# Where the large SBUF tiles of a two-layer encoder kernel begin: a 1696-byte filler, and one small tile moved to another pool

## The chip, the cores and the metric

The program runs on one core of a Trainium2 chip. The metric is device time in microseconds (us): the kernel before takes 2171.83 us, the median of three runs (2171.77 to 2172.46). A core has TensorE (PE in the profile; its weight loads are shown apart, as PEld), VectorE (DVE), ScalarE (ACT), GpSimd (POOL) and SyncE (SP), which here only issues DMAs. SBUF is the on-chip memory that all of them read; a tile of SBUF has 128 partitions, and its place is an address within each partition. This change is about that address.

## The reference

An encoder trunk of two layers over one sequence of 256 tokens and 2048 channels, in float32. Each layer is a token mixer and a gated feed-forward block, each behind an RMSNorm with gain, and with shift, scale and gate from a conditioning vector c:

```python
mod = silu(c) @ w_ada[i] + b_ada[i]          # 6 x 2048 values per layer: sh1 sc1 gt1 sh2 sc2 gt2
h = rmsnorm(x, g_norm[i, 0]) * (1 + sc1) + sh1
x = x + gt1 * (gmlp(h) if i == 0 else gqa(h))
h = rmsnorm(x, g_norm[i, 1]) * (1 + sc2) + sh2
x = x + gt2 * conv_ffn(h)                    # 2048 -> 2 x 5632 -> three-tap conv, gelu gate -> 2048
out = rmsnorm(x, g_final)
```

The gMLP mixer multiplies h by a 2048 x 4096 matrix, mixes tokens in chunks of 128 and multiplies by 2048 x 2048. The attention mixer has 16 query heads and 4 key/value heads of width 128, with a norm of each head and rotary positions.

## The kernel before

All activations lie transposed: 128 channels on the partitions, the 256 tokens along the row, 16 blocks of channels. Weights come from HBM in pieces of mostly 128 x 2048 float32 (1 MB), and every product is made from two parts of each factor, a rounded one and its remainder, both of type float32r: `weight` (L175) loads a piece into a `raw` tile, ScalarE writes the rounded part `hi` (L185), VectorE the remainder `lo` (L186), in chunks of 1024 columns. Activations are split alike: `make_h` (L267) writes the normed input as `hhi` and `hlo`, and `split_f` (L280) writes each 256-token block of an inner activation as `fhi` and `flo`. A product of a 128 x 128 weight block with a 128 x 256 activation block is then three matmuls (`prod_b`, L204), and the third partner, lo times lo, is left out:

```python
mm(out, whi, xhi, start, False)      # mm: T.matmul(out, lhsT=weight, rhs=activation), L202
mm(out, whi, xlo, False, False)
mm(out, wlo, xhi, False, stop)
```

The first operand is the stationary one, loaded into the array by a weight load before each matmul, the second is the moving one, streamed through. In the feed-forward up products (PSUM tiles `pfa`, `pfc`, `pf`) and in the u half of the gMLP (`pu`) the moving operand is a 256-column slice of `hhi` or `hlo`; in the down products (`pd`) and in the output products of the mixers (`po`, `pw`) it is a tile `fhi` or `flo`. Three products have the roles the other way round: in `pv`, `pk` and `pq` 128 columns of `hhi` or `hlo` are stationary and 512 columns of `hi` or `lo` are moving.

Between these, VectorE also makes the 192 columns of `mod` (`ada`, L133: a 1 MB piece of w_ada times a broadcast of silu(c), summed along the row), as the function `pump` hands them out with the weights. `rstd_bcast` (L237) makes 1/rms at the start of each of the five norms, with a small tile `r` of two values per partition. The Tile framework orders the instructions by priority and sets the semaphores; each pool reuses its buffers in turn, and an instruction that writes a reused buffer waits for the last reader.

Pools are laid out one behind the other in the order in which they are opened (L60 to L65): `const` (single small tiles, x, cond_bc), `raws` (5 x 8192 bytes per partition), `his` and `los` (5 x 4096 each), `hbuf` (`hhi` and `hlo`, 16384 each), `tmp` (`ht` 2 x 1024, `acc` 2048, `sqj` 2048, `r` 2 x 32), and, opened anew for each mixer, the pool of `fhi` and `flo` (1024 each) and a scratch pool. A tile takes at least 32 bytes and is padded to a multiple of 32. The const pool begins 128 bytes past a multiple of 1024 (the framework's own constants) and is 30,784 bytes long, so that `raws` begins at 192 past a multiple of 1024. Since all tiles from there to `tmp` are multiples of 1024, all of raw, hi, lo, hhi and hlo begin at 192 past a multiple of 1024 too; the two buffers of r add 64, and fhi and flo begin at 256 past one. Slices of 128 columns are 512 bytes, those of 256 columns 1024 bytes.

Of the kernel before, what the change touches and what calls it, by code (L numbers as in the profile page):

```python
# [9 lines left out]
F32 = mybir.dt.float32  # L10
# [5 lines left out]
P = 128  # L16
# [3 lines left out]
TC = S // P  # L20
# [18 lines left out]
RB = 5  # L39
FB = 18  # L40
HW = 1024
PARTS = (16, 16, 12)
SH1, SC1, GT1, SH2, SC2, GT2 = range(6)

# [2 lines left out]
def kernel(  # L47
# [10 lines left out]
    V, A, G, T, Q = nc.vector, nc.scalar, nc.gpsimd, nc.tensor, nc.sync  # L58

    const = ctx.enter_context(tc.tile_pool(name="const", bufs=1))  # L60
# [8 lines left out]
        return cur["ps"].tile([P, 512], F32, tag=tag or cur["tag"], name=name, bufs=cur["bufs"][tag or cur["tag"]])  # L69

    def phase(stack, name, nf, bufs={"ps": 8}, tag="ps", rt="ps"):
        """pools that live for one mixer: PSUM banks, split activations, scratch"""
        cur["ps"] = stack.enter_context(tc.tile_pool(name=name + "_ps", bufs=1,
                                                     space=bass.MemoryType.PSUM, reuse_waits="tile"))
        cur["bufs"], cur["tag"], cur["rt"] = bufs, tag, rt
        cur["f"] = stack.enter_context(tc.tile_pool(name=name + "_f", bufs=nf, reuse_waits="tile"))
        cur["scr"] = stack.enter_context(tc.tile_pool(name=name, bufs=1, reuse_waits="tile"))
        return cur["scr"]
# [1 line left out]
    def raw_tile(name):  # L80
        return raws.tile([P, 2048], F32, tag="raw", name=name)

# [1 line left out]
    def small(name, shape, src=None):  # L84
        t = const.tile(shape, F32, tag=name, name=name)
        if src is not None:
            Q.dma_start(t, src)
        return t
# [19 lines left out]
    mod = small("mod", [P, DEPTH, 6 * NB])  # L108
    gs = small("gs", [P, DEPTH * 2, NB])

# [1 line left out]
    cond = small("cond", [P, NB])  # L112
    A.activation(cond, cT, AF.Exp, scale=-1.0)
    V.tensor_scalar(out=cond, in0=cond, scalar1=1.0, scalar2=None, op0=ALU.add)
    V.reciprocal(cond, cond)
    V.tensor_tensor(out=cond, in0=cond, in1=cT, op=ALU.mult)
    cond_bc = small("cond_bc", [P, D])
    c_st = ExitStack()
    cur["ps"] = c_st.enter_context(tc.tile_pool(name="c_ps", bufs=2, space=bass.MemoryType.PSUM, reuse_waits="tile"))
    cur["tag"], cur["bufs"] = "ps", {"ps": 2}  # L120
# [8 lines left out]
        A.copy(cond_bc[:, b * S:(b + 1) * S], pb[:, :S])  # L129
    c_st.close()  # L130

# [1 line left out]
    def ada(l, vec, j):  # L133
        m = vec * NB + j
        w = raw_tile(f"ada{l}_{m}")
# [21 lines left out]
        while it not in done:  # L157
            pump_one()

# [1 line left out]
    cnt = [0]  # L161
    pend = []

# [43 lines left out]
        mm(out, whi, xlo, False, False)  # L207
        mm(out, wlo, xhi, False, stop)

# [1 line left out]
    accs = {}  # L211

    def square_into(name, j, src):
# [1 line left out]
            square_(name, j, src)  # L215

    def square_(name, j, src):
        """sum of squares over the blocks of x, two blocks at a time; the last block goes to the tensor engine"""
        if j < NB - 2 and j % 2 == 0:
            return  # L220
        if j < NB - 2:
            src, n = x[:, j - 1:j + 1, :].rearrange("p j t -> p (j t)"), 2 * S
        else:
            n = S
        if j == 1:
            accs[name] = tmp.tile([P, 2 * S], F32, tag="acc", name=f"acc_{name}", bufs=1)
            A.activation(accs[name], src, AF.Square)
            return
        s = tmp.tile([P, 2 * S], F32, tag="sqj", name=f"sq_{name}{j}", bufs=SQB)[:, :n]
        A.activation(s, src, AF.Square)  # L230
        if j < NB - 1:
            V.tensor_tensor(out=accs[name][:, :n], in0=accs[name][:, :n], in1=s, op=ALU.add)
        else:
            a = accs[name]
            accs[name] = (a[:, S:], a[:, :S], s)

    def rstd_bcast(name, keep):  # L237
        """1 / rms of every token over all partitions: a PSUM tile, and a copy in SBUF if it is kept for long"""
        pm = bank(f"pm_{name}", cur["rt"])
        r = tmp.tile([P, TC], F32, tag="r", name=f"r_{name}")  # L240
        dg = tmp.tile([P, S], F32, tag="ht", name=f"dg_{name}")
        pr = bank(f"pr_{name}", cur["rt"])
        for i, a in enumerate(accs[name]):
            for t in range(TC):
                T.matmul(pm[:, t:t + 1], lhsT=a[:, t * P:(t + 1) * P], rhs=mean_w, start=i == 0 and t == 0,
                         stop=i == 2, skip_group_check=True)
        with tc.high_priority():
            V.tensor_scalar(out=r, in0=pm[:, :TC], scalar1=EPS, scalar2=None, op0=ALU.add)
            G.tensor_tensor(out=r, in0=r, in1=neghalf[:, :TC], op=ALU.pow)
            for t in range(TC):  # L250
                V.tensor_scalar(out=dg[:, t * P:(t + 1) * P], in0=ident, scalar1=r[:, t:t + 1],
                                scalar2=None, op0=ALU.mult)
                T.matmul(pr[:, t * P:(t + 1) * P], lhsT=ones, rhs=dg[:, t * P:(t + 1) * P], start=True, stop=True)
            if not keep:
                return pr[:, :S]
            R = cur["scr"].tile([P, S], F32, tag="R", name=f"R_{name}", bufs=1)
            A.copy(R, pr[:, :S])
        return R
# [32 lines left out]
            V.scalar_tensor_tensor(out=x[:, j, :], in0=src, scalar=mcol(l, vec, j), in1=x[:, j, :],  # L291
                                   op0=ALU.mult, op1=ALU.add)

# [1 line left out]
    def gmlp(l, rstd):  # L295
        with ExitStack() as st:
            gm = phase(st, "gm", NB)
# [87 lines left out]
    def gqa(l, rstd):  # L385
        with ExitStack() as st:
# [28 lines left out]
                        mm(pk[t][n], hlo[:, kb, ts_], w(n * 512, 512)[0], False, kb == NB - 1)  # L415

            def rope(nm, ps2, cs):
                """un-normalised rotation of four heads and 1/rms of each; ps2: banks per t-chunk"""
                ss = at.tile([P, TC * 4], F32, tag="qss", name=f"ss{cs}", bufs=2)
                rot = [at.tile([P, 512], F32, tag="p", name=f"rot{cs}{t}", bufs=PB) for t in range(TC)]  # L420
                for t in range(TC):
                    src = ps2[t]
                    for h in range(4):
                        s = at.tile([P, P], F32, tag="qsq", name=f"qsq{cs}{t}{h}", bufs=2)
                        A.activation(s, src[:, h * P:(h + 1) * P], AF.Square,
                                     accum_out=ss[:, t * 4 + h:t * 4 + h + 1])
                    s4 = src.rearrange("p (h d) -> p h d", h=4)
                    V.tensor_tensor(out=rot[t].rearrange("p (h d) -> p h d", h=4), in0=s4,
                                    in1=tabs[nm + "c"][:, t:t + 1, :].broadcast_to([P, 4, P]), op=ALU.mult)
                    sw = at.tile([P, 512], F32, tag="sw", name=f"sw{cs}{t}", bufs=1)  # L430
                    s5 = src.rearrange("p (h a c f) -> p h a c f", h=4, a=2, c=2)
                    sw5 = sw.rearrange("p (h a c f) -> p h a c f", h=4, a=2, c=2)
                    t5 = tabs[nm + "s"][:, t, :].rearrange("p (a c f) -> p a c f", a=2, c=2)
                    for c in range(2):
                        V.tensor_tensor(out=sw5[:, :, :, c, :], in0=s5[:, :, :, 1 - c, :],
                                        in1=t5[:, :, c, :].unsqueeze(1).broadcast_to([P, 4, 2, 32]), op=ALU.mult)
                    V.tensor_tensor(out=rot[t], in0=rot[t], in1=sw, op=ALU.add)
                V.tensor_scalar(out=ss, in0=ss, scalar1=1.0 / P, scalar2=EPS, op0=ALU.mult, op1=ALU.add)
                G.tensor_tensor(out=ss, in0=ss, in1=neghalf, op=ALU.pow)
                return rot, ss  # L440
# [110 lines left out]
    def ffn(l, rstd, nxt, defer):  # L551
        with ExitStack() as st:
# [7 lines left out]
                return b[:, :S], b[:, S:]  # L560

            def epilogue(i, src):
                """three-tap convolution along the tokens of both halves, then gelu(g) * val, split"""
                t = ff.tile([P, 2 * S], F32, tag="t", name=f"t{l}_{i}", bufs=2)
                cols = (i, NPAIR + i)
                for a, o, n in zip(src, halves(t), cols):
                    A.activation(o, a, AF.Identity, bias=cb[:, l, n:n + 1], scale=cw[:, l, 1, n:n + 1])
                for tap, frm, to in ((0, slice(0, S - 1), slice(1, S)), (2, slice(1, S), slice(0, S - 1))):
                    for a, o, n in zip(src, halves(t), cols):
                        V.scalar_tensor_tensor(out=o[:, to], in0=a[:, frm], scalar=cw[:, l, tap, n:n + 1],  # L570
                                               in1=o[:, to], op0=ALU.mult, op1=ALU.add)
                A.activation(t[:, :S], t[:, :S], AF.Gelu)
                V.tensor_tensor(out=t[:, :S], in0=t[:, :S], in1=t[:, S:], op=ALU.mult)
                return split_f(f"f{l}_{i}", t[:, :S])
# [126 lines left out]


def _cols(a, *lead):
    """(..., n*128) -> [128, ..., n]"""
    n = a.shape[-1] // P
    a = a.reshape(*a.shape[:-1], n, P)
    return np.moveaxis(a, -1, 0)


def _nblock(w):  # L710
    """(K, N) -> [N/128][128 k][K/128, 128 n]: the blocks of one column block side by side"""
    K, N = w.shape
    return w.reshape(K // P, P, N // P, P).transpose(2, 1, 0, 3).reshape(N // P, P, -1)

# [75 lines left out]
```

## Time and profile before

| what | before |
|---|---|
| median of 3 runs | 2171.83 us |
| profiled execution, first to last instruction | 2173.2 us |
| instructions | 39151 |
| PE busy | 2099.9 us (97%), 16328 matmuls |
| DVE busy | 1706.8 us (79%) |
| ACT busy | 1019.5 us (47%) |
| POOL busy | 16.6 us (1%) |
| DMA | 580.62 MB, mean 267 GB/s |
| mean granted TensorE clock | 0.980 |

The profiled execution's own time is its span, 2173.2 us. Busy time of an engine is the union of its instructions' times; matmuls overlap each other, so the duration of one (280 ns) is not what it costs: that is the distance from one start to the next. A busy PE of 97% therefore says that PE seldom waits, not that each matmul takes as little as it could.

### The profile page before, as it was taken

To read this page: it belongs to the slowest core of one execution; us is meant where nothing else is said; L and a number is where in the kernel's file an instruction comes from. 1 tells how busy PE (TensorE), PEld (TensorE's weight loads), DVE (VectorE), ACT (ScalarE), POOL (GpSimd) and SP (SyncE) were. 2 spreads that over 40 slices of the span, in tenths; PEclk is the share of its full clock that TensorE was granted. 3 is DMA by queue.
4 is the path that set the end of the run, shared out by engine and by line. 5 is a ranking of instruction groups with operands and counts; after the bars stand their busy time and mean duration, and the time that the engine had idled before them with its cause. 6 is when DMAs were issued, how large, how long until landed. Compare 5 with 4: busy or idle time off the path is not lost.

```text
span 2173.2 us, 39151 instructions
## 1 busy us (share of the span) xinstructions
PE 2099.9 (97%) x16328; PEld 2037.8 (94%) x16328; DVE 1706.8 (79%) x2291; ACT 1019.5 (47%) x1501; POOL 16.6 (1%) x15
## 2 busy tenths in 40 slices
PE   6889998999999999999999999899999999999997
PEld 4669998999999999999988789899999999999997
DVE  8989888889988989889985677876978566655665
ACT  3343444446544554345455554443653445434542
POOL 0000000000000000000000000000000000000000
PEclk7999999999999999999999999899999999999999
DMA  9999997885798889988976346677558655555542
GB/s 370 405 376 360 343 335 275 338 356 201 282 356 326 324 327 336 335 324 309 338 251 224 119 177 242 218 272 296 192 179 320 229 184 178 192 181 188 174 159 95
DMA packets 85137, 580.62 MB, mean 267 GB/s; under 512 B 9952, under 2 KB 11488, under 8 KB 25056
## 3 DMA queue, kind: packets, MB, share of 16 engines
q1 hardware_dynamic: 84960, 578.12, 71.6%
q8 instruction: 128, 2.10, 0.4%
q14 instruction: 49, 0.40, 0.1%
HBM read 575.99 MB, written 2.10 MB: 266 GB/s over the span
## 4 chain that ended last, share of the span: by engine, by line
PE 54%; issue 36%; DVE 7%; ACT 1%; DMA 1%; POOL 0%; SPq 0%; POOLq 0%; DVEq 0%; ACTq 0%
PE pf L202 18%; PE pd L202 11%; PE po L202 4%; PE pu L202 4%; PE pfc L202 4%; DVE ada L137 4%; PE pw L202 3%; PE pk L202 3%; PE pq L202 3%; DVE lo L186 2%; PE pfa L202 2%; PE pqo L506 1%; PE psc L477 0%; DMA ada<-in_wada 0%; ACT hi L185 0%
## 5 line engine op out<-in xcount | busy, mean ns | idle before, releaser
L185 ACT CAST hi<-w 128x1024 fp32r<-128x1024 f32 x740 | 740.1, 1008 | 929.9 <-PE pf L202 360.7
L186 DVE TENSOR_TENSOR lo<-w,hi 128x1024 fp32r<-128x1024 f32 x740 | 859.6, 1170 | 358.6 <-ACT hi L185 353.1
L202 PE MATMUL pf<-hhi_f,lo 128*128 128x256 f32 x2144 | 606.8, 283 | 0.0
L202 PE MATMUL pf<-hhi_f,hi 128*128 128x256 f32 x2144 | 606.8, 283 | 0.0
L202 PE MATMUL pf<-hlo_f,hi 128*128 128x256 f32 x2144 | 606.8, 283 | 0.0
L137 DVE CUSTOM_DVE_ANT_0 ada<-ada,cond_bc,bada 128x2048 f32<-128x2048 f32 x192 | 449.3, 2346 | 24.2 <-DMA ada<-in_wada 24.0
L202 PEld LDWEIGHTS pf<-hhi_f,hi 128*128 128x128 f32 x2144 | 411.6, 192 | 0.0
L202 PEld LDWEIGHTS pf<-hhi_f,lo 128*128 128x128 f32 x2144 | 411.6, 192 | 0.0
L202 PEld LDWEIGHTS pf<-hlo_f,hi 128*128 128x128 f32 x2144 | 411.6, 192 | 0.0
L202 PE MATMUL pd<-fhi_f,hi 128*128 128x256 f32 x1408 | 392.1, 280 | 0.0
L202 PE MATMUL pd<-flo_f,hi 128*128 128x256 f32 x1408 | 391.6, 279 | 0.0
L202 PE MATMUL pd<-fhi_f,lo 128*128 128x256 f32 x1408 | 391.2, 279 | 0.0
L202 PEld LDWEIGHTS pd<-fhi_f,lo 128*128 128x128 f32 x1408 | 264.1, 188 | 0.0
L202 PEld LDWEIGHTS pd<-fhi_f,hi 128*128 128x128 f32 x1408 | 263.6, 188 | 0.0
L202 PEld LDWEIGHTS pd<-flo_f,hi 128*128 128x128 f32 x1408 | 263.1, 187 | 0.0
L202 PE MATMUL pfc<-hhi_f,hi 128*128 128x256 f32 x448 | 126.1, 283 | 0.0
L202 PE MATMUL pfc<-hlo_f,hi 128*128 128x256 f32 x448 | 126.1, 283 | 0.0
L202 PE MATMUL pfc<-hhi_f,lo 128*128 128x256 f32 x448 | 125.5, 283 | 0.0
L570 DVE SCALAR_TENSOR_TENSOR t<-pf,cw,t 128x255 f32<-128x255 f32 x240 | 101.7, 474 | 0.0
L202 PEld LDWEIGHTS pfc<-hhi_f,hi 128*128 128x128 f32 x448 | 85.8, 192 | 0.0
L202 PEld LDWEIGHTS pfc<-hlo_f,hi 128*128 128x128 f32 x448 | 85.8, 192 | 0.0
L202 PEld LDWEIGHTS pfc<-hhi_f,lo 128*128 128x128 f32 x448 | 85.4, 192 | 0.0
(187 smaller groups left out, 2844.6 us busy)
## 6 DMA issues: line engine op xcount, KB each, us to landing
ada<-in_wada SPq DMA_DIRECT2D x192, 1024.0 KB, 6.6
w<-in_wup SPq DMA_DIRECT2D x134, 1024.0 KB, 4.8
w<-in_wdn SPq DMA_DIRECT2D x64, 1024.0 KB, 4.9
w<-in_wup SPq DMA_DIRECT2D x48, 896.0 KB, 5.5
w<-in_wdn SPq DMA_DIRECT2D x32, 768.0 KB, 4.7
w<-in_wv SPq DMA_DIRECT2D x16, 1024.0 KB, 7.1
w<-in_wu SPq DMA_DIRECT2D x16, 1024.0 KB, 7.1
w<-in_wout SPq DMA_DIRECT2D x16, 1024.0 KB, 5.3
```

The source lines that it names most:

```text
L137: V.tensor_tensor_reduce(out=w, in0=w, in1=cond_bc, op0=ALU.mult, op1=ALU.add, scale=1.0, scalar=bada[:, l, m:m + 1], accum_out=mod[:, l, ...
L185: A.copy(hi[:, :n], w[:, c:c + n])
L186: V.tensor_tensor(out=lo[:, :n], in0=w[:, c:c + n], in1=hi[:, :n].bitcast(F32), op=ALU.subtract)
L202: T.matmul(out, lhsT=a, rhs=b, start=start, stop=stop, skip_group_check=True)
L506: T.matmul(po, lhsT=va[:, kc, g * P:(g + 1) * P], rhs=ps_[h][:, kc, :], start=kc == 0, stop=kc == TC - 1)
L570: V.scalar_tensor_tensor(out=o[:, to], in0=a[:, frm], scalar=cw[:, l, tap, n:n + 1], in1=o[:, to], op0=ALU.mult, op1=ALU.add)
```

## The change

A tile `filler` of 424 float32 (1696 bytes) is added at the end of the const pool, of which one column is set to zero by VectorE, since a tile must be written. The tile `r` of each of the five norms goes from the pool `tmp`, where two buffers were used in turn, to the const pool, as five tiles of their own. Nothing else that is executed changes; docstrings and comment lines are left blank.

```diff
@@ -39,6 +39,7 @@
 HW = 1024
+FILL = 424
 PARTS = (16, 16, 12)
...
@@ -108,13 +109,15 @@
     cond_bc = small("cond_bc", [P, D])
+    filler = small("filler", [P, FILL])
+    V.memset(filler[:, 0:1], 0.0)
     c_st = ExitStack()
...
@@ -235,9 +238,9 @@
         pm = bank(f"pm_{name}", cur["rt"])
-        r = tmp.tile([P, TC], F32, tag="r", name=f"r_{name}")
+        r = const.tile([P, TC], F32, tag=f"r_{name}", name=f"r_{name}")
         dg = tmp.tile([P, S], F32, tag="ht", name=f"dg_{name}")
```

The const pool becomes 30,784 + 1696 + 5 x 32 = 32,640 bytes long; with the 128 bytes ahead of it that is 32 x 1024, and `raws`, `his`, `los` and `hbuf` begin at multiples of 1024. `tmp` is now 2048 + 2048 + 2048 bytes, and so `fhi` and `flo` begin at multiples of 1024 as well.

## Rows read from the trace of the kernel before

**Rows 1.** The page, engines: busy us (share of the span) and number of instructions
```profile
PE 2099.9 (97%) x16328; PEld 2037.8 (94%) x16328; DVE 1706.8 (79%) x2291; ACT 1019.5 (47%) x1501; POOL 16.6 (1%) x15
```
**Rows 2.** Windows: span, busy us (instructions) of PE, PEld, DVE, ACT, POOL, clock, DMA
```profile
27.00:145.00 118.00, 99.39 (x374) 75.24 (x375) 117.46 (x140) 40.50 (x50) 0.00 (x0) 0.90 1.01 403
161.00:250.00 89.00, 86.55 (x719) 85.85 (x718) 83.77 (x105) 39.22 (x59) 0.00 (x0) 1.00 0.89 351
651.00:835.00 184.00, 184.00 (x1535) 184.00 (x1535) 165.84 (x216) 91.23 (x125) 0.00 (x0) 1.00 0.87 324
1041.00:1105.00 64.00, 64.00 (x546) 64.00 (x545) 61.42 (x83) 30.08 (x42) 0.00 (x0) 1.00 0.94 355
```
**Rows 3.** Chain that ended last, in order of time, 165 to 1110 us: start, us, what
```profile
171.52 80.95 PE pu L202 x672
252.47 87.52 PE po L202 x743
...
474.71 86.40 PE pf L202 x720
561.11 90.45 PE pd L202 x768
651.56 184.32 PE pf L202 x1536
```
**Rows 4.** Groups by line and shape: count, busy us, mean ns; one of each three
```profile
L202 PE MATMUL pf<-hhi_f,hi 128*128 128x256 f32 x2144 | 606.8, 283 | 0.0
L202 PE MATMUL pd<-fhi_f,hi 128*128 128x256 f32 x1408 | 392.1, 280 | 0.0
L202 PE MATMUL pfc<-hhi_f,hi 128*128 128x256 f32 x448 | 126.1, 283 | 0.0
L202 PE MATMUL pw<-fhi_o,hi 128*128 128x256 f32 x256 | 72.5, 283 | 0.0
L202 PE MATMUL pu<-hhi_a,hi 128*128 128x256 f32 x256 | 72.4, 283 | 1.5 <-DVE v L367 1.5
L202 PE MATMUL po<-fhi_y,hi 128*128 128x256 f32 x256 | 71.6, 280 | 0.0
L202 PE MATMUL pfa<-hhi_f,hi 128*128 128x256 f32 x224 | 63.7, 295 | 5.2 <-ACT hhi_f L276 5.2
L202 PE MATMUL pv<-hi,hhi_a 128*128 128x512 f32 x128 | 50.8, 450 | 16.5 <-ACT hhi_a L276 16.2
L202 PE MATMUL pk<-hi,hhi_b 128*128 128x512 f32 x96 | 38.7, 403 | 1.1 <-ACT hhi_b L276 1.1
L202 PE MATMUL pq<-hi,hhi_b 128*128 128x512 f32 x96 | 38.9, 407 | 2.3 <-ACT qsqq L425 2.3
L202 PEld LDWEIGHTS pf<-hhi_f,hi 128*128 128x128 f32 x2144 | 411.6, 192 | 0.0
L202 PEld LDWEIGHTS pd<-fhi_f,hi 128*128 128x128 f32 x1408 | 263.6, 188 | 0.0
```
**Rows 5.** Timeline of PE at full clock, two matmuls nine apart: start, us, what
```profile
1139.33 0.39 PE L202 MATMUL pk<-hi,hlo_b 128*128 128x512 f32 x1
...
1141.37 0.39 PE L202 MATMUL pk<-hi,hlo_b 128*128 128x512 f32 x1
```
**Rows 6.** Timeline of PE at half clock, and the window's clock
```profile
144.08 0.63 PE L202 MATMUL pv<-lo,hhi_a 128*128 128x512 f32 x1
...
144.93 0.63 PE L202 MATMUL pv<-lo,hhi_a 128*128 128x512 f32 x1
...
144.00:145.50 1.50, 1.50 (x5) 1.13 (x4) 1.50 (x1) 1.48 (x2) 0.00 (x0) 0.50 0.99 415
```
**Rows 7.** Timeline, 13 merged 128-column float32 matmuls, a weight load each
```profile
161.82 1.61 PE L365 MATMUL pg<-ws,v 128*128 128x128 f32 x13
```
**Rows 8.** Groups by line: the small instructions that the change touches or resembles
```profile
L105 DVE MEMSET mean_w<- 128x1 f32 x1 | 0.1, 59 | 0.0
L249 POOL TENSOR_TENSOR r_ff<-r_ff,neghalf 128x2 f32<-128x2 f32 x2 | 3.4, 1714 | 291.8 <-DVE r_ff L248 291.8
```

## The prediction

> **What bounds the kernel now.** I read the engines' shares first, then the chain that ended last, then the windows. PE is busy 97% of the span [rows 1], and in the long stretches of the two feed-forward blocks it is busy all the time, with no idle time in front of its matmuls [rows 2, 4]. The exception is the first product, `pv` (27 to 145 us), where VectorE is busy 117.46 of 118 us and PE 99.39 [rows 2]. Elsewhere VectorE follows closely in the first layer: 165.84 of 184 us, 83.77 of 89, 61.42 of 64 [rows 2]. So outside `pv` time is the number of matmuls times the distance from one start to the next, and that distance is what a change of address could move.
>
> The chain gives this distance, since it merges back-to-back matmuls. 720 of `pf` take 86.40 us, 1536 take 184.32 us: 120.00 ns each, both times. 768 of `pd` take 90.45 us: 117.77 ns each. 743 of `po` take 87.52 us: 117.79 ns; `pu` is near `pf`, 80.95 us for 672 = 120.46, a few stalls included [rows 3]. All four have the same shape, 128 x 256 against a 128 x 128 weight block, and all their weights come from hi and lo. What differs is the moving operand: hhi or hlo, which begin at 192 past a multiple of 1024 bytes, in `pf` and `pu`; fhi or flo, which begin at 256 past one, in `pd` and `po`. The groups show the same split: a matmul of `pf` or `pfc` lasts 283 ns with a weight load of 192 ns, one of `pd` or `po` 280 ns with 188 ns [rows 4].
>
> For the 512-column matmuls the two starts 1139.33 and 1141.37 are nine matmuls apart: 2.04 / 9 = 226.7 ns [rows 5]. At half clock two starts lie two matmuls apart, 144.08 to 144.93: 425 ns for 512 columns, so 212.5 at full clock with nothing added, and 106 for 256 columns [rows 6]. I use 213.3 and 106.7, 512 and 256 columns at 2.4 GHz. What a matmul takes beyond its columns is then 13.3 ns in `pf`, 13.4 ns in `pk`, 11.1 ns in `pd`. It is the same for 256 and for 512 columns, so it belongs to the start of a matmul (or to its weight load) and not to the stream. At the stream's own pace (1024 bytes in 106.7 ns, 9.6 bytes per ns) 13.3 ns is the time of 128 bytes: as if a stream that begins 64 bytes past a multiple of 128 (192 is one) had to read one unit of 128 bytes more, 9 in place of 8, 17 in place of 16. 9 x 13.33 = 120.0 and 17 x 13.33 = 226.7 are the measured distances. For `pd`, which begins at a multiple of 128, 8 units would be 106.7; it takes 117.8, so something else limits it, and that other limit would show in `pf` as soon as the extra unit is gone. This is the reading that I forecast by. It rests on two start addresses and is not forced by them.
>
> **The change part by part.**
>
> The filler's memset is one more VectorE instruction; the like one on `mean_w` takes 59 ns [rows 8]. It costs between 0 and 0.06 us once. I take 0.
>
> The five r tiles of their own remove a wait for the buffer's last reader two norms earlier, long past; POOL's power on r takes 1.7 us before and after [rows 8]. Nothing comes or goes: 0. No DMA, queue or wait is added, and the order of the large work has no reason to change; were the scheduler to order a few instructions differently at the norms, I would expect tenths of a us of either sign.
>
> VectorE, ScalarE and the DMAs read and write the same shapes at other addresses. For them no row before shows a start other than 192 or 256 for the large tiles, so the bounds are a gain or loss of a few ns on each of 740 splits per engine; it is hidden by PE except in `pv` with its 32 pairs of splits, where 5 ns each would be 0.2 us. I take 0.
>
> The moving slices of hhi and hlo (`pf` 3 x 2144, `pfc` 3 x 448, `pfa` 3 x 224, `pu` 3 x 256 = 9216 matmuls [rows 4]) go from 192 to 0 past 1024. Bounds: the column time 106.7 ns below (a gain of 13.3 x 9216 = 123 us), 120.0 above if nothing is won; a loss here would need 0 to be worse than 192. The nearest row is `pd`, 117.77 ns, a start at a multiple of 128. I take that: 2.23 ns x 9216 = 20.6 us. Some 50 of them run at half clock at the start of the feed-forward blocks (`pfa` lasts 295 rather than 283 ns on the mean [rows 4]), where the extra disappears: 20.4 us.
>
> The moving tiles fhi and flo (`pd` 3 x 1408, `po` and `pw` 3 x 256 each = 5760) go from 256 to 0. Bounds: 106.7 ns below (64 us gained), 120.0 above (12.8 us lost, the second rival). I take 117.77 as before: 0.
>
> The 960 matmuls of 512 columns (`pv` 384, `pk` and `pq` 288 each [rows 4]) get an aligned stream too: at most 2.2 ns each if their extra falls from 13.3 to 11.1, nothing in `pv`, which VectorE bounds, and little of `pq`, which waits on the attention. 0.6 us.
>
> The stationary blocks go from 64 past a multiple of 128 to a multiple of 128. Nothing before shows such a weight load beside such a stream. Bounds: the other 11.1 ns of each matmul (the third rival) and a loss as in the second. I take 0.
>
> Sum: 20.4 + 0.6 = 21.0 us off the profiled execution's 2173.2 us, 2152.2. The median of the runs is 1.4 us below the profiled execution, so 2150.8 us. VectorE doesn't become the bound: `pf` from 651 to 835 us would shrink to 180.6 us, with 165.84 of VectorE's work in it.
>
> **Where a page says otherwise.** The distance at full clock is 120.0, 117.77 and 226.7 ns [rows 3, 5]. The Trainium skill, "TensorE: Matmul & The Clock Gate", section "Back-to-back issue gap", puts the gap of a single matmul at N / 2.4 + 2.5 ns: an estimate of 109 ns for 256 columns and 216 ns for 512. The trace disagrees by 9 to 11 ns per matmul; if the addresses were all that stands between the two, the sum by the page's figure would be an estimate of 149 us less (10.8 x 9216 + 8.6 x 5760 ns), which the third rival below holds in the terms of a row.
>
> **The rivals.**
>
> *Slower: the distance between the two addresses counts, not each one's alignment.* In `pf`, `pu` and `pk` the stationary and the moving operand both begin at 192 past 1024 (the stationary ones also at 704), so they lie a multiple of 512 bytes apart, and all three pay 13.3 ns. In `pd` and `po` the moving one lies 64 bytes further, and they pay 11.1 ns. If weight load and stream, which run side by side, get into each other's way when they lie a multiple of 512 apart, the change takes the 64 bytes away, and `pd`, `po` and `pw` fall to 120.0 ns: 2.23 x 5760 = 12.8 us, of which some 0.2 in `pw` lie beside waits on the attention. It decides from the first `po` on: 2171.8 + 12.6 = 2184.4 us. For it speaks that it explains the rows with no second limit, and that the weight load is 4 ns longer where the matmul is slower [rows 4]; against it, that 13.3 ns being just 128 bytes of stream is then chance.
>
> *No change: neither address counts.* The 2.23 ns would come from something that the filler leaves alone, such as hhi being slices of one large tile and fhi tiles of their own, or which part of SBUF they lie in. Then 2171.9 us. That the change doesn't do what it says comes to the same time, but the sum of the pool's tiles gives 32 x 1024 exactly. Against it: `pu` and `pf`, and `po` and `pd`, agree within each pair over different mixers. The Trainium skill says the like: "SBUF — State Buffer", section "Who interferes with whom", has PE read stationary and moving operands through two ports of its own and wait for nobody, and its "Specifications (TRN2)" give lines of 16 bytes, which both kernels' starts respect. By it the four products would not differ, and they do [rows 3].
>
> *Much faster: the rest of the extra is an alignment's price too,* of the stationary blocks, which are off by 64 bytes in every product shown. The nearest floor is `pg`: its 13 matmuls of 128 columns, bound by a weight load each, lie (1.61 - 0.28) / 12 = 111 ns apart [rows 7]. At 111 ns: 9 x 9216 + 6.8 x 5760 = 122 us, with some 3 us more from `pk` and `pq`, and some 5 us lost where VectorE has less room than that [rows 2], in `pu` and the last `pd` of layer 0: about 120 us, 2052 us. Half of it, 2112 us, is as likely as all. Against it: the weight load of `pd` is not shown waiting, and 188 ns is the shortest of the groups.
>
> **How the numbers follow.** Forecast 0.37, the slower rival 0.35, much faster 0.16, no change 0.12. Faster by over 0.2% (4.3 us, about what a measurement can tell from no change): 0.37 + 0.16 = 0.53; within 0.2%: 0.12; slower: 0.35. The forecast alone would be 2146 to 2157 us (the 512-column term from 0 to 2 us, a few us for what starting addresses of 0 do to fhi and flo). The range takes in the slower rival with 3 us for `pk` and `pq`, up to 2188, and the weaker half of the much faster one, down to 2112; about 0.1 is left out.
>
> **What would show it.** In the chain the 720 matmuls of `pf` take 84.8 us instead of 86.40, with weight loads of 188 ns, and 768 of `pd` stay at 90.45. If `pd` grows to 92.2 with weight loads of 192 ns while `pf` stays, the slower rival holds; if both stand still, the address is not it; if both fall towards 80 and 85 us, it is the weights' alignment. A different order of the instructions at the norms, or a stretch where VectorE is now waited for, would make the sum wrong without touching these.

## The result: slower, by the amount of the first rival

The changed kernel takes 2184.64 us, the median of four runs (2184.05 to 2187.21), beside 2172.14 us for the kernel before on the same chip (2171.77 to 2172.68): a ratio over the runs of 1.0061, with a 95% interval of 1.0047 to 1.0076. The forecast was 2150.8 us; the first rival, *the distance between the two addresses counts*, had put it at 2184.4. The profiled execution took 2185.03 us, of which 2183.3 from first to last instruction.

In the chain of the kernel after, in order of time (start, us, what), these are the pieces that answer to [rows 3]:

```profile
168.84 80.95 PE pu L205 x672
249.79 89.17 PE po L205 x743
...
474.25 86.40 PE pf L205 x720
560.64 92.16 PE pd L205 x768
652.80 184.32 PE pf L205 x1536
```

`pf` takes 86.40 us for 720, to the hundredth what it took before, and `pu` 80.95 for 672. `po` went from 87.52 to 89.17 for 743, `pd` from 90.45 to 92.16 for 768: both are now 120.0 ns from start to start, like `pf`. The attention's output product, which [rows 3] don't show, follows: in the chain of before 434 of `pw` from 1318.59 us take 51.13 us, 117.8 ns each; after, 554 of them take 120.0.

```profile
1318.59 51.13 PE pw L202 x434
```

```profile
1323.00 66.48 PE pw L205 x554
```

The groups of the page after, by line and shape (count, busy us and mean ns of one, idle before), answer to [rows 1] and [rows 4]:

```profile
PE 2109.7 (97%) x16328; PEld 2048.0 (94%) x16328; DVE 1706.7 (78%) x2292; ACT 1018.6 (47%) x1501; POOL 16.6 (1%) x15
...
L205 PE MATMUL pf<-hhi_f,hi 128*128 128x256 f32 x2144 | 606.8, 283 | 0.0
...
L205 PEld LDWEIGHTS pf<-hhi_f,hi 128*128 128x128 f32 x2144 | 411.6, 192 | 0.0
...
L205 PE MATMUL pd<-fhi_f,hi 128*128 128x256 f32 x1408 | 396.4, 283 | 0.0
...
L205 PEld LDWEIGHTS pd<-fhi_f,hi 128*128 128x128 f32 x1408 | 269.6, 192 | 0.0
```

A matmul of `pd` lasts 283 ns instead of 280 and its weight load 192 instead of 188; the rows of `pf` are the same to the last digit. VectorE has one instruction more and 0.1 us less to do, and the instructions of PE, ScalarE, POOL and the DMA queue stand in the same order as before. So nothing was waited for that was not waited for before: 5760 matmuls began 2.23 ns later after each other, 12.8 us. The medians differ by 12.5.

The two profiled spans differ by only 10.1 us. The other 2.7 us lie ahead of all this: `pu` begins at 168.84 us after and at 171.52 before [rows 3]. That start lies between 168.86 and 170.70 us in five of the six further chains shown below (in the sixth, with 64 bytes ahead of all four, `pu` is interrupted there), in no order that goes with an address; in `pv`, which runs until then, the granted clock was a little higher (0.92 from 27 to 145 us, [rows 2] have 0.90). So the profiled execution of before was a long one for its kernel: wherever both are on record, a run's time is 1.6 to 2.0 us above its span from first to last instruction, so that the median of 2172.14 us goes with a span of some 2170.3 us and not of 2173.2.

### The profile page after: what moved, and what is told of

Same layout as the page of the kernel before. It is cut to its first block, busy times and chain, and to the rows that moved or that the text cites. A ratio compares the mean times of both kernels' runs of the same rounds, so it can differ in the third digit from the quotient of the medians.

```text
span 2183.3 us, 39151 instructions
## 1 busy us (share of the span) xinstructions
PE 2109.7 (97%) x16328; PEld 2048.0 (94%) x16328; DVE 1706.7 (78%) x2292; ACT 1018.6 (47%) x1501; POOL 16.6 (1%) x15
## 4 chain that ended last, share of the span: by engine, by line
PE 55%; issue 36%; DVE 7%; ACT 1%; POOL 0%; DMA 0%; SPq 0%; POOLq 0%; DVEq 0%; ACTq 0%
PE pf L205 18%; PE pd L205 11%; PE po L205 4%; PE pw L205 4%; PE pu L205 4%; PE pfc L205 4%; DVE ada L140 3%; PE pk L205 3%; PE pq L205 3%; DVE lo L189 2%; PE pfa L205 2%; PE pqo L509 1%; PE psc L480 0%; PE psc L502 0%; ACT hi L188 0%
## 5 line engine op out<-in xcount | busy, mean ns | idle before, releaser
L205 PE MATMUL pd<-flo_f,hi 128*128 128x256 f32 x1408 | 397.2, 283 | 0.0
L205 PE MATMUL pd<-fhi_f,lo 128*128 128x256 f32 x1408 | 396.9, 283 | 0.0
L205 PEld LDWEIGHTS pd<-flo_f,hi 128*128 128x128 f32 x1408 | 270.0, 192 | 0.0
L205 PEld LDWEIGHTS pd<-fhi_f,lo 128*128 128x128 f32 x1408 | 269.8, 192 | 0.0
L205 PEld LDWEIGHTS pd<-fhi_f,hi 128*128 128x128 f32 x1408 | 269.6, 192 | 0.0
```

Source lines behind the costliest of these rows:

```text
L205: T.matmul(out, lhsT=a, rhs=b, start=start, stop=stop, skip_group_check=True)
```

## The experiments

The theory on trial is now the rival's: what counts is how far the moving operand lies from the weight block, and the address of neither by itself. d stands below for the address of the moving operand less that of the weight block, in bytes and with whole multiples of 256 left off (the fourth experiment shows that they don't count). Before, d is 0 in `pf`, `pfc`, `pfa`, `pu` and 64 in `pd`, `po`, `pw`; after, it is 0 in all. Against it stand: the filler (weights and hhi now at other places), the alignment of fhi and flo by itself, and the move of `r` by some way other than the 64 bytes that it gave up.

One more rival can be settled by the two traces alone: that the moving operand meets not PE's own weight load but VectorE, ScalarE or a DMA, which fill `hi`, `lo` and `raw` meanwhile. In stretches in which VectorE and ScalarE are idle for over nine tenths of the distance from one start to the next and no DMA packet is under way, before has 121 distances of `pf` with a mean of 120.0 ns and 90 of `pd` with 117.8; after has 127 and 116, all of 120. These are the means of the whole products (worked out from the traces' records), so none of those three makes the difference; what is left is PE's own two operands.

**64 bytes ahead of fhi and flo alone.** To the changed kernel:

```diff
     tmp = ctx.enter_context(tc.tile_pool(name="tmp", bufs=2))
+    fpad = tmp.tile([P, 16], F32, tag="fpad", name="fpad", bufs=1)
+    V.memset(fpad[:, 0:1], 0.0)
```

> The changed kernel with 64 bytes of pad ahead of the tiles fhi and flo alone: they begin at 64 past a multiple of 1024, weights and hhi, hlo stay at 0. Distance theory (a matmul costs 120.0 ns when its moving operand lies a multiple of 512 bytes from the weight blocks, 117.8 when it lies 64 further): pd, po and pw go back to 117.8 ns, pf stays at 120.0; 12.7 us off the changed kernel's 2184.6, so 2171.9 us, level with the kernel before. Alignment theory (that of the forecast, a start off a multiple of 128 costs): fhi and flo are now off it, so pd is at 120.0 or worse, 2184.6 us or more.

Measured: 2170.84 us, 0.9994 of the kernel before (0.9985 to 1.0004). The chain of this kernel:

```profile
473.89 86.40 PE pf L207 x720
560.29 90.45 PE pd L207 x768
```

The whole loss is gone, with `pd` back at 90.45 us, and `pf` untouched. (In this kernel's profile some 600 matmuls of `pw` and 356 of `pd` are faster still, by 4.4 ns each or 4.2 us, for a reason that the last section takes up; why the median nevertheless lies only 1.3 us below that of before I can't place.) fhi and flo begin at 64 past a multiple of 1024 here and at 256 past one before: other alignments, the same d of 64, the same 117.77 ns.

**64 bytes ahead of hhi and hlo alone.** The filler is cut to 296 floats, so that weights begin 512 bytes earlier; `hpad` of 16 floats stands ahead of hhi, and 112 floats ahead of fhi bring that one back to a multiple of 512:

```diff
-FILL = 424
+FILL = 296
...
     hbuf = ctx.enter_context(tc.tile_pool(name="hbuf", bufs=1))
+    hpad = hbuf.tile([P, 16], F32, tag="hpad", name="hpad")
+    V.memset(hpad[:, 0:1], 0.0)
     tmp = ctx.enter_context(tc.tile_pool(name="tmp", bufs=2))
+    fpad = tmp.tile([P, 112], F32, tag="fpad", name="fpad", bufs=1)
+    V.memset(fpad[:, 0:1], 0.0)
```

> The changed kernel with hhi and hlo alone 64 bytes further than a multiple of 512 from weights and fhi, flo (which stay at a multiple of 512; the filler is 512 bytes shorter to make room). Distance theory: pf, pfc, pfa and pu fall from 120.0 to 117.8 ns, 720 of pf in 84.8 us, pd stays at 120.0; 9216 x 2.23 = 20.5 us off 2184.6, so 2164 us. The products pk, pq, pv with hhi, hlo as the stationary operand move by at most 2 us. Alignment theory: pf stays at 120.0 or gets worse, 2184.6 us or more.

Measured: 2167.61 us, 0.9978 (0.9969 to 0.9988). The two products have changed places, in the chain and in the weight loads:

```profile
472.84 84.80 PE pf L209 x720
557.64 92.17 PE pd L209 x768
649.80 180.91 PE pf L209 x1536
...
1119.81 59.97 PE pk L209 x257
```

```profile
L209 PEld LDWEIGHTS pf<-hhi_f,hi 128*128 128x128 f32 x2144 | 402.3, 188 | 0.0
...
L209 PEld LDWEIGHTS pd<-flo_f,hi 128*128 128x128 f32 x1408 | 270.0, 192 | 0.0
```

180.91 us for 1536 is 117.78 ns. This is the 84.8 us in `pf` that the prediction had hoped for, and it comes from taking hhi *off* the alignment. What is dearer than I had expected is `pk`: 59.97 us for 257 is 233.3 ns where it was 226.7 [rows 5]. There the roles are the other way round (hhi is the weight block, d is -64), and the 64 bytes cost 6.7 ns for 512 columns. On the 576 matmuls of `pk` and `pq` that is at most 3.8 us, and the measured time is 3.6 us above the expected 2164. (`pv`, the third product of this kind, goes to 233 ns as well, where VectorE and not PE sets the time.)

**64 bytes ahead of all four.** The changed kernel with `hpad` alone, which shifts fhi and flo as well:

```diff
     hbuf = ctx.enter_context(tc.tile_pool(name="hbuf", bufs=1))
+    hpad = hbuf.tile([P, 16], F32, tag="hpad", name="hpad")
+    V.memset(hpad[:, 0:1], 0.0)
```

> The changed kernel with hhi, hlo, fhi and flo all 64 bytes further than a multiple of 1024 from the weights. Distance theory: both gains, 2184.6 - 12.7 - 20.5 = 2151.4 us, 1.0% below the kernel before; if the gains do not add up, another engine (VectorE in the first layer) is the bound. Alignment theory: 2184.6 us or more.

Measured: 2152.94 us, 0.9911 (0.9895 to 0.9927). In its chain both products are at 117.8 ns, and `pk` at 233.3 (53.67 us for 230):

```profile
469.89 84.80 PE pf L207 x720
554.69 90.45 PE pd L207 x768
...
1119.96 53.67 PE pk L207 x230
```

The two gains add up (the dearer `pk` and `pq` and some 600 faster matmuls of `pw`, 2.7 us, nearly cancel), and this is near the forecast's time, reached by the opposite address: 64 past a multiple of 1024 for everything that I had wanted at 0.

**A row of distances in one kernel.** The filler at 296 floats again, and rows of hhi and hlo 8 floats longer, so that block kb lies 32 bytes further from its weights than the one before:

```diff
-        hts["hi"] = hbuf.tile([P, NB, S], F32R, tag="hhi", name=f"hhi_{name}")
+        hts["hi"] = hbuf.tile([P, NB, S + 8], F32R, tag="hhi", name=f"hhi_{name}")[:, :, :S]
```

and the same for hlo.

> A map in one run: the rows of hhi and hlo are 1056 bytes instead of 1024, so that block kb begins 32 x kb bytes past a multiple of 512 from the weights, for kb 0 to 15; fhi and flo stay at a multiple of 512. Distance theory: within each group of pf, pfc and pu the distance from start to start varies with kb, 120.0 at kb 0 and 117.8 at kb 2 (64 bytes), and takes other values elsewhere; the curve over 0 to 480 bytes tells whether 64 is the best distance. Alignment theory: 117.8 or less at kb 0, 4, 8, 12 (multiples of 128) and 120 or more between. If a start at 32 past 64 matters for itself, odd and even kb differ.

A single run, 2173.45 us. In `pfc` each block kb is used by 42 matmuls in a row, and after the first few the distances repeat in a short pattern (5 matmuls at 128, 8 at 224). The mean over whole repeats among the last 24, in layer 0, worked out from the trace's starts:

| d of kb 0 to 7 | 0 | 32 | 64 | 96 | 128 | 160 | 192 | 224 |
|---|---|---|---|---|---|---|---|---|
| ns | 120.0 | 117.8 | 117.8 | 120.0 | 118.7 | 117.4 | 117.8 | 118.3 |

kb 8 to 15, 256 bytes further on, give the same eight values to 0.1 ns, and so does layer 1, mostly to the last nanosecond of the pattern: at 0 every distance is 120, at 96 they go 116, 123, 119, 121, 116, 125, at 64 they stay between 117 and 119. So d counts modulo 256 bytes, not 512 as the rival had it, and it makes 120.0 at 0 and 96 and 117.4 to 118.7 elsewhere. No rule of alignment to 32, 64 or 128 gives that row: 96 is as dear as 0, and 128 is not.

**The filler alone.** The kernel before with the filler and with `r` left in `tmp`, so that weights and hhi begin at 864 past 1024, fhi at 928 (d of 0 and 64, as before):

```diff
     cond_bc = small("cond_bc", [P, D])
+    filler = small("filler", [P, FILL])
+    V.memset(filler[:, 0:1], 0.0)
```

> The kernel before with the filler alone; r stays in tmp. Weights, hhi and hlo begin at 864 past a multiple of 1024 (96 past one of 128), fhi and flo at 928, still 64 bytes further than the weights. Distance theory: pf 120.0, pd 117.8 ns, the time of the kernel before, 2172 us: the filler does nothing by itself. Alignment theory: all starts are off a multiple of 128, pd at 120.0 or more, 2184 us or more.

Measured: 2169.54 us, 0.9982 (0.9973 to 0.9992). **The move of r alone,** without a filler, so that everything begins at 352 past 1024:

```diff
-        r = tmp.tile([P, TC], F32, tag="r", name=f"r_{name}")
+        r = const.tile([P, TC], F32, tag=f"r_{name}", name=f"r_{name}")
```

> The kernel before with r in the const pool alone, no filler. Weights, hhi, hlo, fhi and flo all begin at 352 past a multiple of 1024; the 64 bytes of r between hlo and fhi are gone. Distance theory: pd, po and pw go from 117.8 to 120.0 ns, 2172.1 + 12.6 = 2184.7 us: the whole loss from 64 bytes, with nothing aligned. A theory by which the alignment to 1024 did the harm: 2172 us.

Measured: 2184.25 us, 1.0057 (1.0040 to 1.0074). First the chain with the filler alone, then that with the move of `r` alone:

```profile
472.03 86.40 PE pf L205 x720
558.43 90.45 PE pd L205 x768
```

```profile
474.35 86.40 PE pf L202 x720
560.75 92.16 PE pd L202 x768
```

The kernel without a filler is the changed kernel, piece for piece, with every large tile 96 bytes past a multiple of 256. The one with the filler is the kernel before. So the alignment at 1024 does nothing that these runs can tell; the whole change of the time is the 64 bytes that `r` used to take between hlo and fhi. That the filler's kernel is 3.9 us faster than before (2173.42 us in these runs) comes, by its profile, mostly from `pw`, told of in the last section.

**The best of both.** As with all four shifted, but hhi and hlo of the attention's input (`b`) at d of 0, since `pk` and `pq` want that:

```diff
+        for part, room, o in (("hi", 16, 0 if name == "b" else 16), ("lo", 48, 48 if name == "b" else 0)):
+            t = hbuf.tile([P, NB * S + room], F32R, tag="h" + part, name=f"h{part}_{name}")
+            hts[part] = t[:, o:o + NB * S].rearrange("p (j t) -> p j t", t=S)
```

(in `new_h`, in place of the two tiles), and `fpad` of 16 floats as in the first experiment.

> As the version with hhi, hlo, fhi and flo all 64 bytes off (2152.9 us), but hhi and hlo of the attention layer's mixer back at a multiple of 256 from the weights, since there the weights are the 512-column moving operand and 64 bytes cost 233.3 in place of 226.7 ns. Distance theory: pk and pq back at 226.7: 6.6 ns x 288 for pk and about half of that for pq, 3 us less, 2150 us. pu, pf, pd, po and pw stay.

Measured: 2149.34 us, 0.9893 (0.9878 to 0.9908). It beats both kernels, and next to the version with all four shifted 3 us less were expected and 3.6 came (between two series of runs). The chain, and a timeline of `pk` (start, duration, what):

```profile
553.29 90.45 PE pd L207 x768
643.74 180.91 PE pf L207 x1536
```

```profile
1139.80 0.84 PE L207 MATMUL pk<-hi,hlo_b 128*128 128x512 f32 x3
...
1141.61 0.62 PE L207 MATMUL pk<-hi,hlo_b 128*128 128x512 f32 x2
```

The starts 1139.80 and 1141.61 are eight matmuls apart (three merged in the first row, five single ones between): 1.81 / 8 = 226 ns, the distance of [rows 5] to the view's hundredths of a us.

**Pairs of distances.** hhi and hlo each at distances of their own, block by block; four raw buffers instead of five make the room, and the kernel waits for DMAs with four, so its time (2182.24 us, a single run) says nothing:

```diff
-RB = 5
+RB = 4
...
+            hts[part] = Blocks(t, [j * 320 + OFFS.get(name, (0, 0))[k] // 4 + 16 * ((j // 4, j % 4)[k] if name[0] == "f" else 0) for j in range(NB)])
```

(`Blocks`, not shown, takes these places, in units of 4 bytes, as the starts of the 16 blocks; OFFS adds 0 in layer 0 and 32 bytes in layer 1.)

> A second map: in the feed-forward block of layer 0 block kb of hhi lies 64 x (kb div 4) bytes and that of hlo 64 x (kb mod 4) bytes past a multiple of 256 from the weights (16 pairs); in layer 1 both 32 more. The raw weights have 4 buffers in place of 5 to make room, so its time says nothing. Read in pfc, where one kb stays for 42 matmuls. Distance theory: 120.0 at (0, 0), 117.8 at (64, 64); if each matmul pays for its own distance from the next weight load, a mixed pair lies between its parts (two thirds hhi's value, one third hlo's); if the stream is one chain, a mixed pair can be lower than both. (0, 0) of layer 1 is 32, 32: 117.8; 96, 96: 120.0.

The same means in `pfc`, layer 0, in ns (hhi down, hlo across; patterns of up to 12 matmuls here, and for (192, 192) only the last 12 matmuls, since a stall lies ahead of them):

| | 0 | 64 | 128 | 192 |
|---|---|---|---|---|
| 0 | 120.0 | 117.8 | 116.7 | 117.8 |
| 64 | 118.9 | 117.8 | 117.8 | 117.0 |
| 128 | 120.0 | 118.9 | 118.7 | 117.8 |
| 192 | 119.2 | 117.8 | 118.3 | 113.3 |

The table isn't the sum of a price for hhi and one for hlo: by rows 0 and 64, hlo at 128 would be 3.3 ns better than at 0, or 1.1. And it isn't a function of the pair: (0, 0), (64, 64) and (128, 128) have the values of the row of distances, but (192, 192) is 113.3 here, after a stall of PE, and 117.8 there; of the pairs that layer 1 of this kernel has, (96, 96) is 120.0 as there, (32, 32) is 116.7 where 117.8 was expected, and (160, 160) is 120.0 against 117.4. No better pair than 64 with 64 follows that I could have relied on; what follows is that the spacing has a history, which the last section takes up.

## Why the prediction was wrong

**What bounds the kernel** held: the time is the number of matmuls times their distance, no other engine came in, and the distances of before were read rightly. The reading of them was wrong.

**The step that failed** is the term of hhi and hlo, "the nearest row is `pd`, 117.77 ns, a start at a multiple of 128. I take that: 2.23 ns x 9216 = 20.6 us", and with it the zero for fhi and flo. Measured: `pf`, `pfc` and `pu` 120.0 as before, 0 us; `pd`, `po` and `pw` 120.0, 12.8 us lost. Both stood on "as if a stream that begins 64 bytes past a multiple of 128 had to read one unit of 128 bytes more". No run shows such a unit: `pf` stayed at 120.0 ns at a start of 0, and paid 117.8 at a start of 64, off the multiple of 128. That 13.3 ns is just 128 bytes at the stream's pace was chance, as the rival's paragraph had said it would have to be. The rows admitted both readings, since each product had one pair of addresses. One thing in them spoke for the rival and was given too little weight: the alignment needed a second, unnamed limit to explain why an aligned `pd` still paid 11.1 of the 13.3 ns, and the rival needed none.

**The 512-column products,** 0.6 us won, were 0: d stayed 0 and the distance stayed. Between the starts 1139.60 and 1141.41 of `pk` after lie eight matmuls, 226 ns each:

```profile
1139.60 0.39 PE L205 MATMUL pk<-lo,hhi_b 128*128 128x512 f32 x1
...
1141.41 0.84 PE L205 MATMUL pk<-hi,hlo_b 128*128 128x512 f32 x3
```

**The stationary blocks,** taken as 0, were 0 on their own: `pf` didn't move when weights and stream both went to a multiple of 1024. That ends *Much faster*, and *No change* falls with `pd`.

**The small edits** were as costed, and so was the correction for matmuls at half clock, to 0.1 us (34 in the trace of before where the prediction put some 50). To take 1.4 us off the profiled span for the median of the runs mixed two measures, span and run time, of two executions; as both before and after were taken from the same median it shifted the forecast by nothing. The filler's memset takes 59 ns, and POOL's power on `r_ff` 1.7 us as in [rows 8]:

```profile
L120 DVE MEMSET filler<- x1: 59/59/59, 1.0 to 1.0; 128x1 f32 x1
```

```profile
L252 POOL TENSOR_TENSOR r_ff<-r_ff,neghalf 128x2 f32<-128x2 f32 x2 | 3.4, 1716 | 292.4 <-DVE r_ff L251 292.4
```

**The rival** had the cause, the place and the size: 12.6 us from `pd`, `po` and `pw`, against 12.5 measured, and its named signs, `pd` at 92.2 us with weight loads of 192 ns while `pf` stays. Its period was off, 256 bytes and not 512, and how weight load and stream would get into each other's way it left open, as the runs do. With 0.35 against 0.37 for the forecast I had little ground to call the direction, and the range held the time only because it reached to the rival; the forecast's own mechanism has no part in that. Beside this stands the Trainium skill, "SBUF — State Buffer", section "Who interferes with whom", by which PE reads its moving operand and its weights through two independent ports and waits for no one at SBUF. As far as other engines go the traces agree, with the same distances from start to start while those are idle; between PE's own two operands they do not, by 2.2 ns on each of 5760 matmuls for a distance of addresses alone.

**What stays open** is why. That weight load and stream meet in something that depends on their addresses modulo 256 fits the runs, except that the same addresses can have more than one pace; it is argued and not shown, since the runs varied addresses only, and none took the weight load away from beside the stream.

## What to carry to other kernels

Padding to a round address isn't an aim in itself: where two operands are read side by side, try the distance between them; 64 bytes of a small tile between two pools were worth 0.6% here without anyone having meant them. Where a row can be read as alignment of one address or as distance of two, say which rows would tell them apart, and prefer the reading that needs no second limit. A pad that helps one product can hurt one with the roles reversed, so look at each product's spacing, not at the time alone.

## What the runs showed that I had not expected

**The preferred distance depends on the product.** With 256 columns 64 beats 0 by 2.2 ns (117.8 against 120.0); with 512 columns and the activations stationary 0 beats -64 by 6.7 ns (226.7 against 233.3). The row of distances holds `pk` too, with d of -32 x kb: 226.7 at 0, 229 at -192, some 232 at -128 and 233.3 to 233.7 at the other five, so that 0, the dearest for 256 columns, is the cheapest there.

**The same addresses have more than one steady spacing.** Five of the kernels have d of 64 in `pw`. Before, 434 of them took 117.8 ns each (shown at the top), and so did the rest. In the other four (the pad ahead of fhi, all four shifted, the filler alone, the best of both) some 600 take less, from the same place in the program on. With the pad ahead of fhi alone, then in the best kernel:

```profile
1301.12 7.54 PE pw L207 x64
...
1317.78 62.80 PE pw L207 x554
```

```profile
1304.52 49.20 PE pw L207 x434
```

62.80 / 554 and 49.20 / 434 are both 113.4 ns, while the 64 earlier ones of the first took 7.54 us, 117.8 each. The timeline of that first kernel (start, duration, what) catches the switch:

```profile
1315.51 0.47 PE L207 MATMUL pw<-fhi_o,hi 128*128 128x256 f32 x1
1315.82 0.28 PE L207 MATMUL pw<-flo_o,hi 128*128 128x256 f32 x1
...
1316.64 0.28 PE L207 MATMUL pw<-fhi_o,lo 128*128 128x256 f32 x1
1316.76 1.02 PE L511 MATMUL pqo<-p,va 128*128 128x256 f32 x4
1317.43 0.47 PE L207 MATMUL pw<-fhi_o,hi 128*128 128x256 f32 x1
1317.74 0.28 PE L207 MATMUL pw<-flo_o,hi 128*128 128x256 f32 x1
...
1320.46 0.28 PE L207 MATMUL pw<-flo_o,hi 128*128 128x256 f32 x1
```

From 1315.82 to 1316.64 lie seven distances of 117 ns. Then `pqo` comes between, and from 1317.74 to 1320.46 there are 24 of 113.3 ns, at the same distances of addresses. `pd` of the same kernel does it at a stall for VectorE:

```profile
1057.77 0.28 PE L207 MATMUL pd<-fhi_f,hi 128*128 128x256 f32 x1
1057.88 0.28 PE L207 MATMUL pd<-flo_f,hi 128*128 128x256 f32 x1
1058.41 0.39 PE L207 MATMUL pd<-fhi_f,lo 128*128 128x256 f32 x1 [0.25 <-DVE lo L191]
1058.64 0.28 PE L207 MATMUL pd<-fhi_f,hi 128*128 128x256 f32 x1
...
1060.00 0.28 PE L207 MATMUL pd<-fhi_f,hi 128*128 128x256 f32 x1
...
1098.98 0.28 PE L207 MATMUL pd<-flo_f,hi 128*128 128x256 f32 x1
1099.42 0.38 PE L207 MATMUL pd<-fhi_f,lo 128*128 128x256 f32 x1 [0.16 <-DVE lo L191]
```

(1060.00 - 1058.64) / 12 = 113.3 ns; the next stall, at 1099.42, ended it, and between 1100.00 and 1101.17 lie ten of 117.7 ns. So a stream that was left alone stayed in its pattern, and a pause could put it into another. With the filler alone some 600 of `pw` ran at 113.3 as well, which at 4.4 ns each is 2.6 of the 3.9 us by which that kernel was faster than before; the other 1.3 I can't place. What picks the pattern after a pause I did not find, nor how to enter the faster one on purpose. Of the five kernels before alone has fhi itself at a multiple of 256, and each has one profile; whether that address, the execution or something else decides, no run shows. Were all 14976 matmuls of 256 columns in the faster pattern, an estimate from these rows is 4.4 ns x 14976 = 66 us less than with all of them at 117.8, of which the best kernel has 2.7, before VectorE's work [rows 2] would be in the way.
